# Activations of a two-layer decoder trunk moved by 128 bytes, to the weights' start address modulo 512

## The chip, the cores and the metric

The kernel runs on one core of a Trainium2 chip. The metric is the device time of one execution in microseconds (us), as the median of three runs. The core has a matrix engine (PE; its loads of stationary operands are listed apart, as PEld), a vector engine (DVE), a scalar engine (ACT), GpSimd (POOL) and SyncE (SP), which issues most of the transfers. SBUF, the memory on the chip, has 128 partitions; an address below is a byte address inside a partition, the same one in all 128.

## What is computed

A decoder trunk in float32 over 256 tokens of width 2048: one even layer (short convolution and RWKV-7), one odd layer (pooling and latent attention), a SwiGLU after each, and a last norm. What matters here is that nearly all arithmetic lies in dense products of activations with weights, and most of the 400 MB that the page counts as read from memory are weights, each used once:

```python
for layer in range(DEPTH):            # DEPTH = 2
    if layer % 2 == 0:
        p = rms_norm(h, ev_norm[j]) @ ev_w_in[j]
        ...                           # convolution, RWKV-7
        h = h + mix @ ev_w_out[j]
    else:
        p = rms_norm(h, od_norm[j]) @ od_w_in[j]
        ...                           # pooling, attention
        h = h + mix @ od_w_out[j]
    h = h + swiglu(rms_norm(h, ffn_norm[layer]), ffn_w_gate[layer],
                   ffn_w_up[layer], ffn_w_down[layer])
return rms_norm(h, final_norm)
```

## The kernel before

Each operand of a dense product is split into two float32r parts, a high part and a low part (the remainder), and a product of the two operands is taken as three matmuls: high by high, low by high, high by low. Activations stand transposed (features on the partitions), in `xh` and `xl` (four tiles each of 4 x 256 columns, made by `xtiles`). Weights are loaded by halves of a block into `w`, and split by quarters of 512 columns into `wh` (ACT, L96) and `wl` (DVE, L97), six buffers each.

Two forms of dense product use them. All their matmuls are recorded at L57, in `mm`:

- `gemm_tok` (tokens on the output's partitions) takes 128 x 128 of the activations as the stationary operand and streams 512 columns of weights past it. A quarter of weights gives six such matmuls. The profile names them `mm<-wh,xh`, `mm<-wh,xl`, `mm<-wl,xh` and writes `128*128 128x512`: in these names the streamed operand stands first, the stationary one second. I call them long products. The SwiGLU's gate and up products and both output projections are of this form; so are the SwiGLU's down products, with `hh` and `hl` (the SwiGLU's inner activations) in place of `xh` and `xl`, and a few in the attention with `lh` and `ll` (the latents).
- `gemm_wt` (features on the output's partitions) takes 128 x 128 of the weights as the stationary operand and streams 256 tokens of activations: `mm<-xh,wh`, `mm<-xl,wh`, `mm<-xh,wl`, `128*128 128x256`, twelve to a quarter. I call them short products. The input projections of both layers are of this form, and, with `lh` and `ll`, the attention's queries and keys. Two tiles at the start go to `sm` in place of `mm`.

The order of all work is written out by the program: the quarters of weights follow one another, and small steps (recurrence, attention heads, transposes, norms) are placed between quarters in their turn. PE runs its queue in that order.

SBUF is given out from the bottom by pools: `const`, then `xs` (four buffers to a tag unless another number is given), then `wp` (`w`, `wh`, `wl`), then one pool for each stage. Inside a pool a tag gets its space at its first use. In `xs` the first tags used are `xh` and `xl`; `dg` (two buffers of 512 bytes a partition, a diagonal matrix for spreading a row), `ssq` (sums of squares, two of 32) and `rstd` (two of 32 with padding) follow. The built program has these start addresses:

| tiles | first address | modulo 512 (all buffers of the tag) |
|---|---|---|
| `xh` | 37024 | 160 |
| `xl` | 53408 | 160 |
| `dg` | 69792 | 160 |
| `w`, `wh`, `wl` | 70944, 87328, 99616 | 288 |
| `hh`, `hl` (SwiGLU) | 120096, 144672 | 288 |
| `lh`, `ll` (latents) | 117088, 121184 | 352 |

Inside the tiles the matmuls step by 512 bytes (128 columns, as stationary operand), 1024 bytes (256 columns, as streamed operand) or 2048 bytes (512 columns), so a product's operands have the offset modulo 512 that their tiles have.

Of the kernel before, what the change touches and what calls it, by code (L numbers as in the profile page):

```python
# [10 lines left out]
F32 = mybir.dt.float32  # L11
# [7 lines left out]
P = 128  # L19
T = 256  # L20
# [31 lines left out]
class Trunk:  # L52
# [12 lines left out]

# [1 line left out]
    def load_next(self):  # L67
        """the next half of a block; its split into parts frees the space of the fourth after it"""
        if not self.blocks:
            return  # L70
        src = self.blocks[0]
        w = self.wp.tile([P, 1024], F32, tag="w", name="w", bufs=WBUFS)
        o = self.half * 1024
        if isinstance(src, list):
            for i in range(2):
                self.nc.sync.dma_start(
                    out=w[:, i * 512 : i * 512 + 512], in_=src[2 * self.half + i]
                )
            end = self.half
        else:  # L80
            self.nc.sync.dma_start(out=w, in_=src[:, o : o + 1024])
            end = o + 1024 == src.shape[-1]
        self.loaded.append((w, 0))
        self.half = 0 if end else 1
        if end:
            self.blocks.pop(0)
# [19 lines left out]
    def quarter(self):  # L106
        """the next 512 columns of weights; what waits in the background moves on"""
        self.fill()
        self.tick()
        return self.pend.pop(0)  # L110

# [1 line left out]
    def later(self, n, fn):  # L113
# [22 lines left out]
    def drain(self, gen=None):  # L136
        """emits the background's steps up to the end of gen"""
        while self.lane and (gen is None or any(g is gen for g in self.lane)):
            self.step()
# [6 lines left out]
    def split(self, dst, src, scale=None):  # L146
        """dst (hi, lo) float32r <- src [* scale per partition]"""
        nc = self.nc
        hi, lo = dst
        if scale is None:  # L150
            nc.scalar.activation(hi, src, AF.Copy)  # L151
            nc.vector.tensor_tensor(out=lo, in0=src, in1=hi.bitcast(F32), op=ALU.subtract)  # L152
        else:
            nc.scalar.activation(hi, src, AF.Copy, scale=scale)
            nc.vector.scalar_tensor_tensor(
                out=lo, in0=src, scalar=scale, in1=hi.bitcast(F32),
                op0=ALU.mult, op1=ALU.subtract,
            )

    def gemm_wt(self, X, n=4, tag="mm"):  # L160
        """[128 columns of W, tok] = W^T X over n quarters of 4 k tiles"""
        out = self.ps(tag)[:, :T]
# [10 lines left out]
    def gemm_tok(self, X, kcs, out=None, stop=True):  # L173
        """out [tok, 512] x 2 halves (+)= X W over the k tiles 4 kc .. 4 kc + 3 of each kc"""
        new = out is None
# [13 lines left out]

# [1 line left out]
    def transpose_nb(self, X, gname, nb):  # L191
        """512 columns of h (token-major) -> x^T parts, with the norm's gain folded in"""
        nc = self.nc
# [38 lines left out]
    def finish(self, ps, nb, ssq, X, gname):  # L232
        """adds a layer's last part to 512 columns of h and turns them into x^T parts"""
        self.add_h(ps, nb, ssq)
        self.later(3, lambda: self.transpose_nb(X, gname, nb))

    def out_proj(self, M, n0, before, gname):
        """h += M W: all but the last blocks ahead of the last heads; before(kc) makes M[kc]"""
        pool = self.xs
# [11 lines left out]
        X = self.xtiles()  # L251
# [4 lines left out]

# [1 line left out]
    def order(self):  # L258
# [27 lines left out]
    def build(self):  # L286
# [4 lines left out]
        with (  # L291
# [11 lines left out]
            self.sin = cp.tile([P, T], F32, name="sin")  # L303
            self.h = cp.tile([P, 2, D], F32, name="h")
            nc.vector.memset(self.mhalf, -0.5)
            nc.vector.memset(self.ones, 1.0)
# [14 lines left out]
    def last(self, HX, kcs, ssq):  # L321
        """the last 512 columns and the final norm, one half of the tokens ahead of the other"""
        nc, a, V = self.nc, self.a, self.nc.vector
# [49 lines left out]
    def sums_tok(self, out, xs, w):  # L373
        """out [tok, ...] = sum of x^T w for both halves of the tokens; x [128, 256]"""
        n = w.shape[-1]
# [7 lines left out]
    def rsqrt(self, out, ps, scale, eps):  # L383
        """out = (scale ps + eps) ** -0.5"""
        n = out.shape[-1]
# [5 lines left out]
    def row_bcast(self, rb, rs):  # L391
        """rb [128, 256] <- rs [tok, 2], each token's value on every partition"""
        nc = self.nc
# [6 lines left out]

# [1 line left out]
    def ffn(self, X, ssq, gname, between=None):  # L402
# [60 lines left out]

# [1 line left out]
    def even_mix(self):  # L465
# [6 lines left out]

        # x^T parts, by pieces that alternate with the first weights
        X = self.xtiles()
# [9 lines left out]
        gmask, blk, smask = cst[:, 0:128], cst[:, 128:256], cst[:, 256:516]  # L484
        # 1/rms, as a row on every partition
        rb = tp.tile([P, T], F32, name="rb0")
# [19 lines left out]

        # space of h until x is loaded there
        hv0, hv1 = self.h[:, 0], self.h[:, 1]
# [41 lines left out]
        def first_tiles():  # L550
            """four column tiles at once, so that x^T is wanted no faster than it comes"""
            warm = self.ps()
# [59 lines left out]
        def spread(out, v):  # L612
            """out [128, tok] <- v [tok, (half, head)], each head on its 64 partitions"""
            vx = ta("vx").rearrange("p (t h n) -> p t h n", t=2, h=2)
# [12 lines left out]
        def open_group(grp):  # L627
            """even heads on partitions 0-63 with rows (B | K), odd heads on 64-127 with (K | B)"""
            g = {}
# [12 lines left out]
        def prep_a(ti):  # L642
            """decays and key norms of two heads"""
            i = ti % 4
# [33 lines left out]
            S.activation(ch(Ei), cum[:, :, 1:65], AF.Exp, scale=KAPPA)  # L678
            # 1 / norm of the keys, [tok, half, head]
            kn = tp.tile([P, 4], F32, tag="kn", name="kn", bufs=2)  # L680
# [7 lines left out]
        def prep_b(ti):  # L688
            """keys, values and the Gram matrices of two heads"""
            grp, i = ti // 4, ti % 4  # L690
# [6 lines left out]
            for w in range(4):  # L697
                nc.tensor.transpose(  # L698
                    pv[:, w * P : w * P + P], v[:, w * 64 : w * 64 + P], self.ident
                )  # L700
            # window w has chunk w on rows 0-63 and chunk w + 1 on 64-127
            pvv = pv.rearrange("p (w h n) -> p w h n", w=4, h=2)
# [41 lines left out]
            S.activation(BKt[:, i], pb.rearrange("p (c n) -> p c n", c=4), AF.Copy)  # L744
            # Gram matrices, rows at s, columns (Z | R) at t
            for hh in range(2):
# [11 lines left out]
                )  # L758
                # N goes to TT, its 32 x 32 diagonal blocks also to DG; its place in G takes Z
                for q in range(2):  # L760
# [12 lines left out]
        def recur(grp):  # L773
            """the recurrence over four chunks of 64 tokens, eight heads at a time"""
            g = groups[grp]
            g2, G, TT, UV, BKt, bv = (g[n] for n in ("g2", "G", "TT", "UV", "BKt", "bv"))
            pend, ZRs = g["pend"], g["ZR"]
            nc.sync.dma_start(out=g2, in_=a["g2"][grp])
            # inverse of I - N on 32 x 32 diagonal blocks, one on each partition
            dN = self.dp.tile([16, P, 32], F32, tag="dN", name="dN")  # L780
# [67 lines left out]
            for c in range(4):  # L848
# [44 lines left out]
                yield GAPS['h3']  # L893
            # group norm, bonus, gate
            ycs, sqs = [], []
# [42 lines left out]

        # dense products with the recurrence's steps in their background
        first_tiles()  # L940
# [40 lines left out]

# [1 line left out]
    def rope_tables(self):  # L983
# [85 lines left out]

# [1 line left out]
    def odd_mix(self, X, rs):  # L1071
# [9 lines left out]

        # latents: gain folded into the parts, 1/rms row kept for after the products
        lat, rows = [], []
# [48 lines left out]

        # pooling mixer's input
        up = tp.tile([P, 4, 16 + T], F32, name="up")
# [4 lines left out]

        # keys, values, queries  # L1140
        kn = tp.tile([P, HEADS, T], F32, name="kn")
# [114 lines left out]
        def slots(b, gap):  # L1256
            """heads in turn, each a step behind the one before it"""
            for h in range(4 * b, 4 * b + (4 if b < 2 else 6)):
# [40 lines left out]
def _wt(w):  # L1299
    """[K, N] -> [N/128, 128, (K/128) * 128]: one stationary column tile to a row block"""  # L1300
    K, N = w.shape
# [3 lines left out]
def _tok(w):  # L1305
    """[K, N] -> [N/512, K/512, 128, 4 * 512]"""
    K, N = w.shape
# [125 lines left out]
```

## Time and profile before

| | us |
|---|---|
| runs | 2301.1, 2294.25, 2289.76 |
| median | 2294.25 |
| span of the profiled execution, first to last instruction | 2288.4 |
| PE busy | 2273.3 (99%) |
| DVE busy | 1371.6 (60%) |
| ACT busy | 1167.5 (51%) |

The span is that of one profiled execution; the page gives no other time for it. The three timed runs lie 1.4, 5.9 and 12.7 us above it. Matmuls are pipelined: a record's own length (390 to 400 ns for a long product) is longer than the distance from its start to the next one's, and it is that distance that adds up to the span. In the chain of work that ended last, a piece such as "PE mm L57 x192" with its length gives that distance as a mean: length by count. In the timeline it can be read from the starts.

### The profile page before, as it was taken

How to read it: one execution, taken by the hardware profiler on the slowest of the kernel's cores; microseconds unless marked ns; L12 is line 12 of the kernel's file. 1: busy time of each engine (PE TensorE's matmuls, PEld its weight loads, DVE VectorE, ACT ScalarE, POOL GpSimd, SP SyncE). 2: the span in 40 equal slices, each digit the busy share in tenths (PEclk: the TensorE clock that was granted, in tenths of full speed). 3: DMA queues.
4: the chain of work that ended last, by engine and by line, in shares of the span. 5: the costliest groups of instructions: out<-in, count | busy, mean ns of one | idle time of the engine just before them, and what ended most of it. 6: DMA issues, size and time to landing. Idle time of an engine off the chain costs nothing.

```text
span 2288.4 us, 33957 instructions
## 1 busy us (share of the span) xinstructions
PE 2273.3 (99%) x12422; PEld 1919.0 (84%) x12422; DVE 1371.6 (60%) x2432; ACT 1167.5 (51%) x2085; POOL 27.2 (1%) x41
## 2 busy tenths in 40 slices
PE   9999999999999999999999999999999999999998
PEld 9999898778888888888888998788888888888886
DVE  7785587558555555555555677665555555555554
ACT  7655464455454444444455545465444444454454
POOL 0000000000000000000000000000000000000000
PEclk9999999999999999999999999999999999999999
DMA  8455236535555555555555553355555555555554
GB/s 302 134 178 166 93 121 194 170 108 182 184 187 187 184 195 193 185 184 185 187 187 186 185 169 126 126 180 197 186 185 184 184 193 193 185 187 187 181 191 155
DMA packets 124680, 405.46 MB, mean 177 GB/s; under 512 B 24896, under 2 KB 25152, under 8 KB 124128
## 3 DMA queue, kind: packets, MB, share of 16 engines
q1 hardware_dynamic: 122896, 398.31, 52.1%
q0 software_dynamic: 896, 3.80, 0.6%
q8 instruction: 97, 1.59, 0.3%
q10 hardware_dynamic: 720, 1.18, 0.1%
q14 instruction: 71, 0.58, 0.1%
HBM read 400.10 MB, written 3.15 MB: 176 GB/s over the span
## 4 chain that ended last, share of the span: by engine, by line
PE 97%; DVE 1%; DMA 1%; ACT 0%; issue 0%; POOLq 0%; POOL 0%; SPq 0%; DVEq 0%
PE mm L57 88%; PE sm L57 7%; PE sm L434 1%; DVE wl L97 1%; PE sm L198 0%; DMA Nb<-dN 0%; DMA dN<-DG 0%; DVE Tb L806 0%; DVE ou L802 0%; PE sm L1239 0%; ACT wh L96 0%; DMA pkt<-pk 0%; PE sm L698 0%; PE sm L741 0%; DVE h L602 0%
## 5 line engine op out<-in xcount | busy, mean ns | idle before, releaser
L97 DVE TENSOR_TENSOR wl<-w,wh 128x512 fp32r<-128x512 f32 x1482 | 1017.3, 691 | 792.5 <-ACT wh L96 774.8
L96 ACT ACTIVATE wh<-w 128x512 fp32r<-128x512 f32 x1482 | 932.4, 631 | 975.7 <-PE mm L57 696.6
L57 PE MATMUL mm<-wh,xh 128*128 128x512 f32 x1664 | 664.4, 399 | 2.2 <-ACT xh L151 2.2
L57 PE MATMUL mm<-wh,xl 128*128 128x512 f32 x1664 | 656.4, 394 | 1.2 <-DVE xl L152 1.2
L57 PE MATMUL mm<-wl,xh 128*128 128x512 f32 x1664 | 523.1, 395 | 0.0
L57 PEld LDWEIGHTS mm<-wh,xh 128*128 128x128 f32 x1664 | 313.7, 189 | 78.3 <-ACT xh L151 2.7
L57 PEld LDWEIGHTS mm<-wl,xh 128*128 128x128 f32 x1664 | 313.2, 188 | 73.7
L57 PEld LDWEIGHTS mm<-wh,xl 128*128 128x128 f32 x1664 | 313.7, 189 | 71.6 <-DVE xl L152 1.5
L57 PE MATMUL mm<-xh,wh 128*128 128x256 f32 x992 | 286.8, 289 | 1.2 <-ACT wh L96 1.2
L57 PE MATMUL mm<-xh,wl 128*128 128x256 f32 x992 | 280.7, 283 | 0.0
L57 PE MATMUL mm<-xl,wh 128*128 128x256 f32 x992 | 280.6, 283 | 0.0
L57 PE MATMUL mm<-wh,hh 128*128 128x512 f32 x704 | 274.5, 390 | 0.0
L57 PE MATMUL mm<-wh,hl 128*128 128x512 f32 x704 | 273.9, 389 | 0.0
L57 PE MATMUL mm<-wl,hh 128*128 128x512 f32 x704 | 220.1, 389 | 0.0
L57 PEld LDWEIGHTS mm<-xh,wh 128*128 128x128 f32 x992 | 187.9, 189 | 4.5 <-ACT wh L96 1.5
L57 PEld LDWEIGHTS mm<-xl,wh 128*128 128x128 f32 x992 | 188.1, 190 | 0.5
L57 PEld LDWEIGHTS mm<-xh,wl 128*128 128x128 f32 x992 | 187.7, 189 | 0.3 <-DVE wl L97 0.2
L57 PEld LDWEIGHTS mm<-wl,hh 128*128 128x128 f32 x704 | 132.1, 188 | 27.5
L57 PEld LDWEIGHTS mm<-wh,hl 128*128 128x128 f32 x704 | 132.2, 188 | 27.3
L57 PEld LDWEIGHTS mm<-wh,hh 128*128 128x128 f32 x704 | 132.1, 188 | 27.2
L228 DVE TENSOR_TENSOR h<-mm,h 128x512 f32<-128x512 f32 x54 | 34.9, 685 | 4.8 <-PE mm L57 4.7
L57 PE MATMUL mm<-lh,wh 128*128 128x256 f32 x120 | 35.4, 295 | 0.0
(256 smaller groups left out, 1278.0 us busy)
## 6 DMA issues: line engine op xcount, KB each, us to landing
w<-f_gate SPq DMA_DIRECT2D x176, 512.0 KB, 3.7
w<-f_up SPq DMA_DIRECT2D x176, 512.0 KB, 3.6
w<-f_down SPq DMA_DIRECT2D x176, 512.0 KB, 3.6
w<-e_in SPq DMA_DIRECT2D x94, 512.0 KB, 3.9
w<-e_out SPq DMA_DIRECT2D x32, 512.0 KB, 3.7
w<-o_out SPq DMA_DIRECT2D x32, 512.0 KB, 3.6
w<-o_in SPq DMA_DIRECT2D x26, 512.0 KB, 3.6
w<-e_in SPq DMA_DIRECT2D x16, 256.0 KB, 6.1
```

The costliest lines, as they stand in the source:

```text
L57: return self.nc.tensor.matmul(out, lhsT, rhs, start=start, stop=stop)
L96: nc.scalar.activation(hi, w[:, sl], AF.Copy)
L97: nc.vector.tensor_tensor(out=lo, in0=w[:, sl], in1=hi.bitcast(F32), op=ALU.subtract)
L228: nc.vector.tensor_tensor(out=hs, in0=ps[t], in1=hs, op=ALU.add)
L434: nc.tensor.transpose(pt[:, i * T + t * P : i * T + t * P + P], ac[t][:, (j + i) * P : (j + i + 1) * P], self.ident,)
```

## The change

Three tags of `xs` are used once before anything else, so that they get the pool's lowest addresses; the tiles made there are not written or read.

```diff
@@ build
             self.cos = cp.tile([P, T], F32, name="cos")
             self.sin = cp.tile([P, T], F32, name="sin")
             self.h = cp.tile([P, 2, D], F32, name="h")
+            for tag, shape in (("dg", [P, P]), ("ssq", [P, 2, 4]), ("rstd", [P, 2])):
+                self.xs.tile(shape, F32, tag=tag, name=tag, bufs=2)
             nc.vector.memset(self.mhalf, -0.5)
...
```

The rest of the diff takes away comments. In the built program every engine has the same instructions in the same order with the same waits; only start addresses differ, and only those of `xs`:

| tiles | modulo 512 before | after |
|---|---|---|
| `xh`, `xl` | 160 | 288 (1152 bytes higher) |
| `dg` | 160 | 160 (now at the pool's start, 37024) |
| `w`, `wh`, `wl`, `hh`, `hl` | 288 | 288 (unmoved) |
| `lh`, `ll` | 352 | 352 (unmoved) |

## Rows read from the trace of the kernel before

**Rows 1.** The page: busy time by engine, and the chain that ended last.

```profile
PE 2273.3 (99%) x12422; PEld 1919.0 (84%) x12422; DVE 1371.6 (60%) x2432; ACT 1167.5 (51%) x2085; POOL 27.2 (1%) x41
PE 97%; DVE 1%; DMA 1%; ACT 0%; issue 0%; POOLq 0%; POOL 0%; SPq 0%; DVEq 0%
```

**Rows 2.** PE's groups by form: count, busy us, mean ns of one, idle before.

```profile
L57 PE MATMUL mm<-wh,xh 128*128 128x512 f32 x1664 | 664.4, 399 | 2.2 <-ACT xh L151 2.2
L57 PE MATMUL mm<-wl,xh 128*128 128x512 f32 x1664 | 523.1, 395 | 0.0
...
L57 PE MATMUL mm<-xh,wh 128*128 128x256 f32 x992 | 286.8, 289 | 1.2 <-ACT wh L96 1.2
...
L57 PE MATMUL mm<-wh,hh 128*128 128x512 f32 x704 | 274.5, 390 | 0.0
...
L57 PE MATMUL sm<-xh,wl 128*128 128x256 f32 x32 | 9.1, 284 | 0.0
```

**Rows 3.** The chain that ended last: start us, us, what (by its count).

```profile
129.83 71.20 PE mm L57 x600
...
524.95 44.62 PE mm L57 x192
...
1019.46 44.79 PE mm L57 x192
...
1156.24 27.22 PE mm L57 x120
...
1360.08 9.89 PE mm L57 x84
```

**Rows 4.** Timeline of long products, stationary xh and xl (first), hh and hl (then).

```profile
628.55 0.40 PE L57 MATMUL mm<-wh,xl 128*128 128x512 f32 x1
628.56 0.19 PEld L57 LDWEIGHTS mm<-wh,xh 128*128 128x128 f32 x1
628.71 0.69 DVE L97 TENSOR_TENSOR wl<-w,wh 128x512 fp32r<-128x512 f32 x1 [0.70 <-ACT wh L96]
628.79 0.39 PE L57 MATMUL mm<-wh,xh 128*128 128x512 f32 x1
628.79 0.19 PEld L57 LDWEIGHTS mm<-wh,xl 128*128 128x128 f32 x1
...
872.48 0.39 PE L57 MATMUL mm<-wh,hh 128*128 128x512 f32 x1
872.48 0.19 PEld L57 LDWEIGHTS mm<-wh,hl 128*128 128x128 f32 x1
872.71 0.39 PE L57 MATMUL mm<-wh,hl 128*128 128x512 f32 x1
```

**Rows 5.** Timeline of long products with the latents as stationary operand.

```profile
1346.23 0.40 PE L57 MATMUL mm<-wh,ll 128*128 128x512 f32 x1
...
1348.56 0.40 PE L57 MATMUL mm<-wh,ll 128*128 128x512 f32 x1
```

**Rows 6.** Timeline of the weight loads in a run of short products.

```profile
160.40 0.19 PEld L57 LDWEIGHTS mm<-xh,wl 128*128 128x128 f32 x1
160.52 0.19 PEld L57 LDWEIGHTS mm<-xh,wh 128*128 128x128 f32 x1
```

**Rows 7.** Busy us (instructions) of stretches; then granted clock, DMA share, GB/s.

```profile
0.00:50.00 50.00, 47.73 (x367) 46.75 (x368) 33.89 (x71) 36.86 (x71) 1.89 (x14) 1.00 0.89 308
100.00:150.00 50.00, 50.00 (x408) 48.35 (x407) 39.05 (x91) 29.21 (x62) 1.23 (x1) 1.00 0.56 174
600.00:700.00 100.00, 100.00 (x440) 81.32 (x439) 54.18 (x79) 48.50 (x78) 0.00 (x0) 1.00 0.54 185
870.00:1000.00 130.00, 130.00 (x571) 106.49 (x570) 69.89 (x102) 62.09 (x100) 0.00 (x0) 1.00 0.57 190
```

**Rows 8.** The chain again, at the end of the even layer's input projection.

```profile
331.95 1.63 PE mm L57 x12
333.59 0.40 ACT TT L766
333.99 0.53 ACT wh L96
...
349.19 6.58 DMA dN<-DG
355.80 0.49 SPq L792
356.34 8.08 DMA Nb<-dN
...
388.81 0.34 DVE xl L152
389.20 11.00 PE mm L57 x40
```

**Rows 9.** PE's products in 340 to 400 us, by form.

```profile
L57 PE MATMUL mm<-xh,wl 128*128 128x256 f32 x118 | 33.3, 283 | 0.0
L57 PE MATMUL mm<-xh,wh 128*128 128x256 f32 x117 | 33.3, 285 | 0.0
L57 PE MATMUL mm<-xl,wh 128*128 128x256 f32 x117 | 33.0, 282 | 0.0
```

## The prediction

> **What bounds the kernel now.** I read the page first, then the chain of work that ended last, then the timeline of single matmuls. The page says that PE is busy for 2273.3 of 2288.4 us and that the chain lies on PE for 97% of the span [rows 1]. So what the change is worth is the change in the distance from one matmul's start to the next, times the count. The busy times cannot give that distance, since a record runs on past the next one's start; the chain can. Its pieces are runs of matmuls with nothing between them [rows 3]:
>
> - long products with `xh` and `xl`: 44.62 / 192 = 232.4 ns each in the first SwiGLU, 44.79 / 192 = 233.3 ns later on;
> - long products with `hh` and `hl`: 27.22 / 120 = 226.8 ns;
> - short products with `xh` and `xl`: 71.20 / 600 = 118.7 ns;
> - short products with `lh` and `ll`: 9.89 / 84 = 117.7 ns.
>
> The first two lines are the same matmul in shape, in type, and in what is done with its weights; a quarter of weights gives six of either. They differ by 5.6 to 6.5 ns. What else could make that difference? The work beside them does not: DVE is busy 54.18 of 100 us beside the first and 69.89 of 130 (the same 54%) beside the second, and transfers run at 185 and 190 GB/s [rows 7]. The place in memory at large does not either: `lh` and `ll` lie in the same region as `hh` and `hl`, and as stationary operands of long products they take (1348.56 - 1346.23) / 10 = 233 ns (ten products start in that stretch, two of the rows between hold two each) [rows 5]. What sorts the three is the offset modulo 512 of the streamed weights (288) against the stationary operand: `hh` 288, no difference, 226.8 ns; `xh` 160, 128 bytes below, 232.4 to 233.3; `lh` 352, 64 above, 233. The timeline shows where the two operands meet: the load of the next stationary operand starts within 0.01 us of the product before it and takes 0.19 of the product's 0.23 us, so PE reads both at once, from the same moment on [rows 4]. That the two reads disturb each other, by an amount that depends on their addresses, is my reading; the rows show the amounts and not the mechanism.
>
> The Trainium skill speaks against this reading. "TensorE: Matmul & The Clock Gate", section "Step-by-step: what each phase is for", says that PE has two independent read ports to SBUF and that a load of weights takes no read bandwidth from the running matmul. By that rule the operands' addresses could not matter, the sum below would be nil and the time 2294; it is the third case below. The trace does not agree: 5.6 ns lie between products that differ in nothing else that I can find.
>
> **The change, part by part.** No instruction is added, removed or moved, and no wait; `w`, `wh`, `wl`, `hh`, `hl`, `lh` and `ll` keep their addresses. `dg` keeps its offset of 160, and `ssq` and `rstd` are a few bytes a partition and no operand of a dense product. So only products with `xh` and `xl` can change, and steps that write those tiles, which start at a multiple of 32 bytes before and after.
>
> *Long products.* 3 x 1664 = 4992 use `xh` or `xl` [rows 2]. After the change their two operands stand to each other as those of the 3 x 704 products with `hh` and `hl` do now. Between the runs of 232.4 and 233.3 I take 232.6, nearer to the first since the later runs alternate between 44.62 and 44.79; the gain is 232.6 - 226.8 = 5.8 ns, and 4992 x 5.8 = 29.0 us. The bounds are 5.6 and 6.5 ns: 28.0 and 32.4 us.
>
> *Short products.* 3 x 992 = 2976 in `mm` and 3 x 32 = 96 in `sm` use them, 3072 in all [rows 2]. No row shows a short product with equal offsets, so this term is bounded from its neighbours. If equal offsets help a short product in the same ratio as a long one, it takes 118.7 x 226.8 / 232.6 = 115.7 ns, a gain of 3.0. If they save a fixed 5.8 ns at each load, it takes 112.9. On the other side, the only two offsets that short products show (128 apart for `xh`, 64 for `lh`) lie 1.0 ns apart, and loads take 0.19 us there while products start every 0.12 [rows 6], so that a load is under way all the time and equal starts need not be the best ones; I let it lose that 1.0 ns, 119.7. I take 115.7, the ratio, because the disturbance must lie within the product, and a short one has half the reads to be disturbed: 3072 x 3.0 = 9.2 us. Bounds: a gain of 17.8, a loss of 3.1.
>
> *What of it is on the path.* In the SwiGLUs all of it: PE is busy for the whole of those stretches, and its feeders have room. A quarter there takes 6 x 232.6 = 1396 ns and would take 1361; DVE's 54% becomes 55%, and 185 GB/s becomes 190, where the first 50 us moved 308 [rows 7]. In the short products DVE is busy 39.05 of 50 us [rows 7], 78%, which becomes 80%: still cover. One stretch gives nothing. From 333.59 to 389.20 us the chain leaves PE for DVE, ACT and a transfer out and back (6.58 and 8.08 us) [rows 8]; PE starts its first long products only when DVE has made `xl`. 352 short products lie in there [rows 9]; 352 x 3.0 = 1.1 us of their gain turns into waiting for DVE. What is late next there is the same DVE queue.
>
> Sum: 29.0 + 9.2 - 1.1 = 37.1 us off the span of 2288.4, that is 2251.3. The median of the runs lies 5.9 above the span, so 2294.25 - 37.1 = 2257.
>
> **The rivals.**
>
> *Only the long products gain.* If the short ones stay at 118.7 the time is 2294.25 - 29.0 = 2265, and at 119.7 it is 2268. For it: short products meet a load all the time, so there may be no offset at which they escape it, and their two known offsets differ by only 1.0 ns. Against it: the same pair of reads is cheaper at equal offsets in the one form where the trace has both.
>
> *Nothing happens.* The 5.8 ns could come from something that goes with the SwiGLU's down products and that I don't see, or the tiles could fail to move. The second is excluded by the built addresses. The first needs a cause that `hh` has and neither `xh` nor `lh` has; the rows on DVE and transfers speak against the two that I can name. Time: 2294, and with a small part of the gain down to 2285.
>
> *Slower.* Equal starts could hurt the short products as much as they help the long ones. The place is the input projections of both layers; the mechanism is that the streamed and the loaded operand, both read without a pause there, start at the same address modulo 512 each time and keep in each other's way through the whole product. It decides from 29.0 us / 3072 = 9.4 ns on, a short product of 128.1 ns. If a short product lost twice what a long one gains, 11.6 ns, it would cost 35.6 us and give 2294.25 + 35.6 - 29.0 = 2301. Against it: offsets change the known products by 1.0 and by 6.5 ns at most, nothing by 9.4.
>
> **How the numbers follow.** Forecast, both gain: 0.72, 2257, its own range 2246 (32.4 + 17.8 - 352 x 5.8 ns = 48.2 off) to 2264. Only the long ones: 0.18, 2265 to 2269 (28.0 - 3.1 = 24.9 off). Nothing: 0.06. Slower: 0.04. From 2246 to 2269 all of the first two cases are held; I add 2 to 3 us at each end, since the runs of one kernel lie 1.4 to 12.7 above the span: 2244 to 2272. A measurement of this kernel can tell about 0.5%, 11.5 us, from no change; both gaining cases are beyond that. Faster 0.90, the same 0.06, slower 0.04.
>
> **What would show it.** In the profile after, runs of 192 long products with `xh` in the chain should take 43.5 us (226.8 ns), with starts 0.23 apart as regularly as with `hh`; the run of 120 with `hh` should stay at 27.2 and the `lh` runs at 117.7 and 233 ns. The run of 600 short products should take 69.4 us at 115.7 ns; 71.2 would mean the first rival, 77 or more the slower one. The wait before the first long product, near 389 us, should be there still and about 1 us longer. If the run of 192 stays at 44.6, my reading of the addresses is wrong.

## The result and the profile after

The changed kernel takes 2268.11 us (median of four runs, 2264.59 to 2271.44) against 2292.01 for the kernel before (four runs, 2289.2 to 2301.1): a ratio of 0.9887, with a 95% interval of 0.9866 to 0.9908. That is 1.1% faster, inside the range given (2244 to 2272) and 11 us above the time given (2257). It is the time of the first rival, "only the long products gain" (2265 to 2269).

The page after, the lines of [rows 1] and the groups of [rows 2] (busy us, mean ns of one, idle before):

```profile
PE 2250.6 (99%) x12422; PEld 1921.0 (85%) x12422; DVE 1371.0 (60%) x2432; ACT 1166.4 (51%) x2085; POOL 27.1 (1%) x41
...
L57 PE MATMUL mm<-wh,xh 128*128 128x512 f32 x1664 | 654.4, 393 | 2.2 <-ACT xh L151 2.2
...
L57 PE MATMUL mm<-wl,xh 128*128 128x512 f32 x1664 | 513.7, 390 | 0.0
...
L57 PE MATMUL mm<-xh,wh 128*128 128x256 f32 x992 | 288.5, 291 | 1.3 <-ACT wh L96 1.3
...
L57 PE MATMUL mm<-wh,hh 128*128 128x512 f32 x704 | 274.5, 390 | 0.0
```

The records of long products with `xh` have fallen from 399 and 395 ns to 393 and 390, those with `hh` stand at 390 as before, and those of short products have risen from 289 to 291. The chain that ended last has the distances themselves (start us, us, what), for the pieces of [rows 3]:

```profile
130.72 72.00 PE mm L57 x600
...
278.94 5.91 PE mm L57 x36
...
529.41 43.54 PE mm L57 x192
...
1059.69 43.54 PE mm L57 x192
...
1148.52 27.22 PE mm L57 x120
...
1353.09 9.89 PE mm L57 x84
...
1533.56 43.54 PE mm L57 x192
```

| from start to start | before | after |
|---|---|---|
| long, `xh` and `xl` | 232.0 to 233.3 ns | 43.54 / 192 = 226.8 |
| long, `hh` and `hl` | 226.8 | 27.22 / 120 = 226.8 |
| short, `xh` and `xl` | 118.7 | 72.00 / 600 = 120.0 |
| short, `lh` and `ll` | 117.7 | 9.89 / 84 = 117.7 |

All runs of 192 now take the same 43.54 us; before they lay between 44.55 and 44.79.

The same starts tell where the 21.1 us between the two spans (2288.4 and 2267.3) went. From the first run of 192 to the first run of 120 the time fell from 1156.24 - 524.95 = 631.29 us to 1148.52 - 529.41 = 619.11, by 12.2; from the second SwiGLU's first run to the end from 2288.4 - 1541.90 = 746.5 to 2267.3 - 1533.56 = 733.7, by 12.8; the down products and the odd layer between them took 0.6 less. (The second SwiGLU begins at 1541.90 us in the chain of before.) The even layer, up to the first run of 192, grew from 524.95 to 529.41, by 4.5 us. By their counts its 384 long products gain 2.2 and its 2448 short ones lose 3.2; another 1.5 us is the piece at 278.94 us, 36 short products in 5.91 us where the kernel before has the same piece in 4.38. The granted clock of that stretch is the reason (busy us by engine, then granted clock, DMA share, GB/s; after, then before):

```profile
278.90:284.90 6.00, 6.00 (x39) 5.87 (x40) 2.57 (x6) 2.82 (x8) 1.01 (x1) 0.72 0.35 122
```

```profile
277.10:281.50 4.40, 4.40 (x38) 4.26 (x38) 2.57 (x6) 2.71 (x8) 1.01 (x1) 1.00 0.43 142
```

The rest lies where the chain leaves PE [rows 8]. From the last piece of 36 short products ahead of it (at 319.47 us before, 323.08 after) to the first long products (389.20, 394.88) it took 69.73 us and takes 71.80, 2.1 more. The transfer out and back there took 6.58 and 8.08 us before; the chain of after has

```profile
352.75 6.88 DMA dN<-DG
...
360.19 9.92 DMA Nb<-dN
```

which is 2.1 us more. That is a difference between executions rather than of the offset: in e1 below, whose products are as long as the changed kernel's, the two took 6.90 and 7.96 us.

### The profile page after: what moved, and what is told of

It reads as the page before. It is cut to its first block, busy times and chain, and to the rows that moved or that the text cites. A ratio compares the mean times of both kernels' runs of the same rounds, so it can differ in the third digit from the quotient of the medians.

```text
span 2267.3 us, 33957 instructions
## 1 busy us (share of the span) xinstructions
PE 2250.6 (99%) x12422; PEld 1921.0 (85%) x12422; DVE 1371.0 (60%) x2432; ACT 1166.4 (51%) x2085; POOL 27.1 (1%) x41
## 4 chain that ended last, share of the span: by engine, by line
PE 96%; DMA 2%; DVE 1%; ACT 1%; issue 0%; SPq 0%; POOL 0%; POOLq 0%; DVEq 0%; ACTq 0%
PE mm L57 87%; PE sm L57 6%; PE sm L436 1%; DVE wl L97 1%; DMA xt<-x 0%; PE sm L198 0%; DMA Nb<-dN 0%; DMA xr<-xT 0%; DMA dN<-DG 0%; DMA pkt<-pk 0%; PE sm L1241 0%; ACT wh L96 0%; PE sm L700 0%; ACT xh L154 0%; PE sm L743 0%
## 5 line engine op out<-in xcount | busy, mean ns | idle before, releaser
L57 PE MATMUL mm<-wh,xh 128*128 128x512 f32 x1664 | 654.4, 393 | 2.2 <-ACT xh L151 2.2
L57 PE MATMUL mm<-wh,xl 128*128 128x512 f32 x1664 | 649.4, 390 | 1.2 <-DVE xl L152 1.2
L57 PE MATMUL mm<-wl,xh 128*128 128x512 f32 x1664 | 513.7, 390 | 0.0
```

Source lines behind the costliest of these rows:

```text
L57: return self.nc.tensor.matmul(out, lhsT, rhs, start=start, stop=stop)
```

## The experiments

Theory A was that the offset modulo 512 between the streamed operand and the one being loaded beside it sets the distance, and nothing else about the addresses. The rival B was that some other property of the place counts. Then there was the question why short products lost. All readings below are pieces of the chain that ended last: the run of 600 short products in the even layer, a run of 192 long ones and a run of 120 with `hh`, whose operands have equal offsets in every kernel. Padding ahead of `w` moves `w`, `wh`, `wl` and all that lies behind them.

### e1: the weights moved instead

```diff
+            self.wp.tile([P, 96], F32, tag="pad", name="pad", bufs=1)
             nc.vector.memset(self.mhalf, -0.5)
```

on the kernel before.

> The activations stay at 160 modulo 512, as before the change; 384 bytes of padding ahead of w move w, wh, wl (and everything allocated behind them) from 288 to 160. Theory A (what counts is the offset modulo 512 between the streamed operand and the one being loaded): as in the changed kernel, 192 long products with xh in 43.5 us, 600 short ones in 72.0, span near 2267. Theory B (what counts is where the activations themselves start, 288 being better for long products than 160): as before, 44.6 and 71.2, span near 2288.

The chain of e1 (start us, us, what, here and below):

```profile
131.24 72.00 PE mm L57 x600
...
532.10 43.55 PE mm L57 x192
...
1151.29 27.22 PE mm L57 x120
```

Both values of the changed kernel, with the activations where they had been. So it is the relation of the two addresses that counts, not the activations' own place. Span 2270.2 us.

### e2: only xl moved

```diff
+            self.xs.tile([P, 4, T], F32R, tag="xh", name="xh")
             for tag, shape in (("dg", [P, P]), ("ssq", [P, 2, 4]), ("rstd", [P, 2])):
```

on the changed kernel: `xh` at 160, `xl` at 288 modulo 512.

> dg, ssq and rstd placed between xh and xl: xl starts at 288 modulo 512, as the weights, xh stays at 160. A gemm_tok quarter streams wh,xh0 wh,xl0 wh,xh1 wh,xl1 wl,xh0 wl,xh1 in this order. Theory A1 (a product is held up by the load of the NEXT stationary operand, which runs beside it): wh,xh products, beside which xl is loaded, become as short as with hh (226.8 ns from start to start, records of 389 to 390 ns), wh,xl and wl,xh products, beside which xh is loaded, stay at 232 to 233 (records 394 to 395). Theory A2 (its OWN stationary operand counts): wh,xl falls to 389 to 390, wh,xh stays. Among short products those that stream xl take 120.0, those that stream xh 118.7, under either.

The chain of e2, then PE's groups by form (busy us, mean ns of one, idle before):

```profile
130.78 71.97 PE mm L57 x600
...
525.72 44.61 PE mm L57 x192
```

```profile
L57 PE MATMUL mm<-wh,xh 128*128 128x512 f32 x1664 | 661.9, 398 | 2.2 <-ACT xh L151 2.2
L57 PE MATMUL mm<-wh,xl 128*128 128x512 f32 x1664 | 657.6, 395 | 1.2 <-DVE xl L152 1.2
L57 PE MATMUL mm<-wl,xh 128*128 128x512 f32 x1664 | 522.2, 395 | 0.0
```

No group fell to 390; the run of 192 took 44.61 us, 232.3 ns, as if nothing had been moved. From start to start, in the trace of e2, `wh,xh` products took 231.8 ns in the mean, `wh,xl` ones 229.3 ahead of another `wh` and 235.6 ahead of a `wl`; none comes down to 226.8. Both A1 and A2 are wrong: one well placed operand in two gives a long product nothing, whether it is loaded beside it or its own. The expectation for short products failed too: with 120.0 for the third of them that stream `xl` and 118.7 for the others, the run of 600 would have taken 71.5 us; it took 71.97, 119.95 ns, so `xl` alone at offset 0 costs them all that `xh` and `xl` together cost. What a product costs depends on more than one pair of addresses. Whether it is two pairs, with its own stationary operand and with the next, or reaches further back, is open.

### e3 to e9: other offsets

With n bytes of padding, as in e1, on the kernel before (e3: 320, e4: 128, e6: 32) or on the changed one (e5: 224, e7: 64, e8: 32, e9: 96). For e3:

```diff
+            self.wp.tile([P, 80], F32, tag="pad", name="pad", bufs=1)
             nc.vector.memset(self.mhalf, -0.5)
```

> The activations at 64 bytes above the weights modulo 512 (160 against 96, by 320 bytes of padding ahead of w), the offset that lh and ll have in every kernel. Theory A: long products with xh as those with lh now, 233 ns (192 in 44.7 us); short ones as with lh now, 117.7 (600 in 70.6 us). If something else than the offset makes lh differ from xh, they stay at one of the two pairs known for xh: 232.6 and 118.7, or 226.8 and 120.0.

The chain of e3:

```profile
128.31 70.67 PE mm L57 x600
...
533.64 44.79 PE mm L57 x192
```

117.8 and 233.3 ns, the values of `lh` and `ll`, which lie elsewhere but at the same offset. The offset decides.

> The activations 256 bytes away from the weights modulo 512. If the pattern repeats every 256 bytes: 226.8 ns for long products (192 in 43.5 us) and 120.0 for short ones (600 in 72.0 us), as in the changed kernel. If every 512 bytes: long ones at 232 to 234 ns, as at the other offsets known (192 in 44.6 to 44.9 us), short ones at 117 to 119.

The chain of e4:

```profile
131.77 72.00 PE mm L57 x600
...
539.52 43.55 PE mm L57 x192
```

The values of offset 0. So 0 and 256 are alike, and from here on I count offsets modulo 256, not modulo 512 as the title and my prediction have it. 0 is the one offset run both ways up to here; e5 to e9, and the kernel before, lie in the upper half (modulo 512 their offsets are 256 more).

> Activations 32 bytes above the weights modulo 256. Offsets 0 and 256 gave the same times and 64 and 128 others, so offsets are now counted modulo 256. If equal starts are a special case (both reads then keep in step), this gives 231 to 234 ns for long products (192 in 44.4 to 44.9 us) and 117 to 119 for short ones (600 in 70.2 to 71.4 us). If the cost grows with the distance, long ones lie between 226.8 and 233.3, near 230, and short ones between 120.0 and 117.6, near 119.

```profile
129.78 70.00 PE mm L57 x600
...
523.35 44.79 PE mm L57 x192
```

116.7 and 233.3 ns; the runs of 192 lie between 44.73 and 44.80 us. For long products a distance of 32 bytes is as bad as one of 128: equal starts are a special case and not the bottom of a slope.

> Activations 96 bytes above the weights modulo 256, between 64 (233.3 and 117.6 ns) and 128 (232.6 and 118.7). If equal starts are the special case: long products 232 to 234 ns, short ones 117 to 119. If the cost has a finer period than 256 that these two happened to miss, one of the forms lies outside these.

```profile
129.86 72.00 PE mm L57 x600
...
573.19 44.98 PE mm L57 x192
```

120.0 and 234.3 ns (the shortest run of 192 took 44.93 us, 234.0). Long ones are at their worst here; short ones as at 0.

> Activations 192 bytes above the weights modulo 256 (64 below). If the sign of the distance does not matter: as at 64, 233.3 ns for long and 117.6 for short products (600 in 70.6 us). If it matters which of the two reads runs ahead: another value, for long ones anywhere from 227 to 236, for short ones from 115 to 120.

The chain of e7:

```profile
127.64 68.01 PE mm L57 x600
...
573.27 43.96 PE mm L57 x192
...
1152.18 27.22 PE mm L57 x120
```

113.4 and 229.0 ns. The sign matters: 64 bytes below is not 64 bytes above. Short products have a best offset too, and it is another one than the long products'.

> Activations 32 bytes below the weights modulo 256. If the sign does not matter: as in e5 at 32 bytes above. If it matters which read runs ahead: the two differ; the smallest pitch of short products over all offsets so far (117.6 at 64) shows then which side to search.

```profile
130.53 70.98 PE mm L57 x600
...
529.32 44.80 PE mm L57 x192
```

118.3 and 233.3 ns (runs of 192: 44.72 to 44.80 us). For short products these are not the values of 32 above, 116.7.

> Activations 160 bytes above the weights modulo 256, between 128 (232.6 and 118.7 ns) and 192 (229.0 and 113.4, the shortest short products so far). If 192 is the middle of a good stretch, 160 gives short products of 114 to 117 ns (600 in 68.4 to 70.2 us) and long ones of 229 to 232. If 192 is a special case as 0 is for the long ones, 160 gives 117 to 120 and 232 to 234.

```profile
129.56 71.19 PE mm L57 x600
...
528.09 44.80 PE mm L57 x192
```

118.7 and 233.3 ns (runs of 192: 44.74 to 44.81 us): 192 is a special value, not the middle of a stretch.

### e10: an offset for each form

On the changed kernel, with `LONG, SHORT = 52, 44`, in elements of 4 bytes:

```diff
-    def xtiles(self):
+    def xtiles(self, short=False):
+        s = SHORT if short else LONG
...
+        xh = [self.xs.tile([P, 4 * T + 64], F32R, tag="xh", name="xh") for _ in range(4)]
+        xl = [self.xs.tile([P, 4 * T + 64], F32R, tag="xl", name="xl") for _ in range(4)]
+        cut = lambda x, k: x[k // 4][:, s + k % 4 * T : s + k % 4 * T + T]
+        return [(cut(xh, k), cut(xl, k)) for k in range(16)]
```

`xtiles(True)` serves the input projections of both layers. To make room, the even layer's `junk` tile takes the tag `solA`, whose tiles are no longer used by then.

> The two forms get offsets of their own: each xh and xl tile has 256 bytes more, and a product's view of it starts further on; products of the long form at 208, of the short form at 176 bytes above the weights modulo 256, 16 bytes to either side of 192. sumsq's junk tile shares the space of the recurrence's solA tile, to make room. If 192 is the middle of a good stretch: short ones at 113 to 115 ns (600 in 67.8 to 69.0 us), long ones at 228 to 231 (192 in 43.8 to 44.4). If 192 is a special case: short ones at 116 or more, long ones at 231 or more.

```profile
129.32 71.55 PE mm L58 x600
...
523.87 44.80 PE mm L58 x192
569.54 44.51 PE mm L58 x192
```

119.3 ns for short products at 176; for long ones at 208 the runs of 192 took 44.49 to 44.80 us, 231.7 to 233.3 ns. 16 bytes beside 192 the gain is gone for short products, and at most 1.6 ns are left of it for long ones.

### e11 and e12: the best offset for each form, beside the change

e11 is e10 with `LONG, SHORT = 0, 48` (0 and 192 bytes), the best values tried; e12 is the changed kernel again.

> As e10, with products of the long form at offset 0 and those of the short form at 192 modulo 256, the two values at which each form was shortest. If the two forms can be set one by one: 192 long products in 43.5 us, 600 short ones in 68.0, and against the changed kernel 3072 x (120.0 - 113.4) = 20.3 us less, near 2248. If what made the short products short at 192 was something else that moved with the padding in e7 (the places of the later tiles), they stay near 118 to 120 and the time near 2268.

The chain of e11:

```profile
41.17 6.66 DMA h<-lora
...
128.34 68.01 PE mm L58 x600
...
280.34 4.21 PE mm L58 x36
...
316.35 4.35 PE mm L58 x36
...
519.66 43.54 PE mm L58 x192
...
1138.77 27.22 PE mm L58 x120
```

> The changed kernel once more, beside e11 on the same chip. Theory A gives again 43.5 us for 192 long products and 72.0 for 600 short ones; its share of the time before should again be near 0.989. How far its executions lie apart shows what the stretches of half clock in the recurrence are worth.

The chain of e12:

```profile
41.52 7.51 DMA h<-lora
...
132.03 71.99 PE mm L57 x600
...
287.31 4.42 PE mm L57 x36
...
324.38 4.42 PE mm L57 x36
...
531.77 43.54 PE mm L57 x192
```

It repeats the values of the changed kernel. The time of both, beside the kernel before:

| | median us (runs) | ratio to before | 95% interval |
|---|---|---|---|
| before | 2296.71 (11) | 1 | |
| e12, the change | 2271.54 (6) | 0.9890 | 0.9869 to 0.9911 |
| e11, 0 and 192 | 2256.24 (4) | 0.9831 | 0.9811 to 0.9851 |

Both forms take the best values tried in one kernel, and e11 beats both the kernel before and the change; the intervals of e11 and e12 don't meet. Between the medians lie 15.3 us, not the 20.3 that I had expected. 352 short products in the stretch that waits for DVE [rows 8, 9] would give back 352 x 6.6 ns = 2.3 us of it. Of the remaining 3 the chains show two parts, as far as two single executions can tell. In the first 50 us both chains run over a transfer (`h<-lora`), so what the 300 or so short products there save, 2.0 us by the count, need not shorten anything. And among the recurrence's small matmuls, between 274 and 320 us of e11, pieces of 36 short products take 4.21 to 4.35 us against 4.42 in e12: 2 to 6 ns a product, not the 6.6 of the long run. The tiles of e11 have 4352 bytes, eight and a half times 512, so that they lie by turns in either half modulo 512; that the values of 0 and 192 come out all the same is a second sign that 256 bytes is the period.

## Why the prediction was right, and where it was off

- **The time** fell outside the range of the case that I held likeliest (both forms gain, 0.72, 2246 to 2264) and into that of the first rival (0.18, 2265 to 2269). The stated range holds 2268 because it spans both cases; the number of the forecast was not borne out.
- **What bounds the kernel** was right: PE stays at 99%, and a change in the distance between matmuls went into the span.
- **Long products** were right to the tenth: 226.8 ns, 5.8 us less for a thousand of them. The sum of 29.0 us for 4992 agrees with what the chain shows where nearly all of them lie: 12.2 and 12.8 us off the two SwiGLUs, with 4224 of the 4992 (4224 x 5.8 ns = 24.5).
- **The reason** was half right. e1, e3 and e4 show that the relation of the two addresses decides, and that the `hh` rows could be read as a preview. But offsets 256 apart are alike (e4), and "the load beside it" is too simple (e2). That it is PE's own two reads that meet is still a reading; the other engines can be ruled out further than I did. DVE and ACT read and write `w`, `wh` and `wl`, which lie at the same offset, but in the trace of before the starts of long products lie 232.6 ns apart in the mean where DVE is busy the whole time and ACT idle (1429 of them) and 232.7 where it is the other way round (1278); after, 226.9 and 226.7. The transfers into `w` are not parted off in this way. Before this change, `xh` lay 128 bytes off, half of 256.
- **Short products** are the term that came out wrong. I had "equal offsets help a short product in the same ratio as a long one", 115.7 ns and 9.2 us gained; they took 120.0, 3072 x 1.3 = 4.0 us lost, just beyond the bound that I had given on that side (119.7). The 12 us between the two (9.2 + 4.0 - 1.1) are the 11 between 2257 and 2268. What the runs show in its place: at equal starts a long and a short product differ by 226.8 - 120.0 = 106.8 ns for 256 columns, 0.417 ns a column, which is one column a cycle at 2.4 GHz, the level granted there (1.00, the number before the last two in the rows at the end of this item). So each pays the same 13.3 to 13.4 ns beyond its columns (213.3 and 106.7 ns) in the mean. It need not be the same cost: from start to start the long ones are even, 226 or 227 ns, while the short ones of the run of 600 go through 117, 118, 120, 121 and 124, each as often as the others, so that their surcharge goes from 10 to 17. My ratio took the surcharge to go with the length; my other guess, a fixed 5.8 ns saved, took the surcharge at the old offset to be the same for both forms, and it was not: 232.6 - 213.3 = 19.3 for a long product, 118.7 - 106.7 = 12.0 for a short one. For the short product the old offset was already the better of the two. Why equal starts, which even out the long products, do not even out the short ones stays open. The stretches of after that hold the run of 600 and runs of 192 (busy us by engine, granted clock, DMA share, GB/s):

```profile
130.00:202.00 72.00, 72.00 (x601) 71.95 (x600) 56.74 (x140) 38.15 (x65) 0.00 (x0) 1.00 0.65 200
600.00:700.00 100.00, 100.00 (x451) 83.02 (x450) 55.23 (x81) 49.77 (x80) 0.00 (x0) 1.00 0.57 190
```

- **The stretch that waits for DVE** behaved as said in kind: PE's first long products wait 2.2 us for ACT's `xh` and 1.2 for DVE's `xl`, before and after. The short products did not get faster, so whether the wait would have grown by the 1 us of the sum was not put to the test here. In e11, where they did, the two waits are 2.2 and 1.2 us again; the chain of e11 leaves PE at other places.
- **Nothing happens and slower**: neither came. The Trainium skill's "TensorE: Matmul & The Clock Gate", section "Step-by-step: what each phase is for", has the load of weights take no read bandwidth from the running matmul. If nothing else is at work, kernels with the same instructions say otherwise here: by address alone long products take 226.8 to 234.3 ns and short ones 113.4 to 120.0. For an isolated matmul at full clock the section "Back-to-back issue gap" of the same page of the Trainium skill gives a gap of N / 2.4 + 2.5 ns, by which I estimate 215.8 and 109.2; no offset tried comes down to either.

## What to carry to other kernels

Where one group of matmuls runs steadily faster than another of the same shape, list the start addresses of the streamed and the stationary operands: here their offset modulo 256 was worth 3% of a matmul of 512 columns and 6% of one of 256. Do not carry a good offset from one form to another: measure it for each, at steps of 32 bytes or finer, in the chain's long runs, where one execution shows tenths of a nanosecond that the total time hides. A tile a little larger than needed, viewed from a shifted start, gives each use its own offset.

## What the runs showed of the hardware

- **Offsets.** Activations against weights, modulo 256 bytes (for 176 and 208 the form that was set there):

| offset | long product, ns | short product, ns |
|---|---|---|
| 0 (after, e1, e4) | 226.8 | 120.0 |
| 32 (e5) | 233.3 | 116.7 |
| 64 (e3) | 233.3 | 117.8 |
| 96 (e6) | 234.0 to 234.3 | 120.0 |
| 128 (before) | 232.0 to 233.3 | 118.7 |
| 160 (e9) | 233.3 | 118.7 |
| 176 (e10) | | 119.3 |
| 192 (e7) | 229.0 | 113.4 |
| 208 (e10) | 231.7 to 233.3 | |
| 224 (e8) | 233.3 | 118.3 |

Only 0 and 192 stand out. These are means over runs in the chain. They are also the even ones where they are short: long products at 0 start 226 or 227 ns apart and short ones at 192 start 113 or 114 apart, while before the long ones went from 228 to 241 and the short ones from 115 to 122. The surcharge of a short product at 192, 113.4 - 106.7 = 6.7 ns, is half of the 13.3 at 0; by the clock granted there that is 16 and 32 cycles, and the long product's at 0 is 32 as well (an estimate, 2.4 GHz times these numbers). Why, no run here shows.

- **Not every short product gains alike.** The 113.4 ns hold in the run of 600. In e11, between 274 and 320 us, pieces of 36 among the recurrence's small matmuls took 4.21 to 4.35 us, 117 to 121 ns a product, against 123 in e12.

- **The granted clock in the recurrence** differs from one execution to the next, and the time of a run goes with it. The six runs of e12 go from 2264.03 us at a mean granted clock of 0.997 to 2275.54 at 0.993. It falls to its lower level, 1.2 GHz, in the stretches in which PE has been going through the recurrence's small matmuls, in other places each time. In e4, whose products are as short as the changed kernel's, it fell more often (0.990 in the mean, against 0.997), and its span is 2277.6 us, 10 more (busy us by engine, granted clock, DMA share, GB/s):

```profile
200.00:270.00 70.00, 70.00 (x706) 62.52 (x705) 26.96 (x54) 25.00 (x50) 2.96 (x4) 0.88 0.26 88
...
440.00:500.00 60.00, 60.00 (x456) 44.96 (x456) 19.16 (x38) 17.43 (x34) 2.52 (x1) 0.86 0.23 76
500.00:600.00 100.00, 99.08 (x460) 80.82 (x459) 75.97 (x152) 60.81 (x117) 1.73 (x3) 1.00 0.51 171
```

So the total of a single execution tells offsets apart by no more than some 10 us; the runs in the chain, which lie in stretches at 1.00, tell them apart to tenths of a nanosecond.
